# Decode attention in a two-branch decoder step: query rows written at the end of the selection, value matmuls handed out at each column chunk

## The chip, the core and the metric

The kernel runs on one core of one Trainium2 chip. The metric is the device time of one execution in microseconds. The core has a matrix engine (TensorE, PE in the profile, with PEld for its weight loads), VectorE (DVE), ScalarE (ACT), GpSimd (POOL) and SyncE (SP), whose queue issues nearly all DMAs here. Each engine runs its own list of instructions in order; semaphores tie the lists together.

## The reference

One layer of a decoder trunk is computed for a prompt of 1024 rows and for 8 sampled rows (one new token for each of 8 sequences with 4096 cached tokens). One input projection feeds an attention branch and an mLSTM branch, whose gated outputs go through one output projection. The prompt's attention and the mLSTM are left out below; the part that the change touches is the sampled rows' sparse attention: an indexer scores all 4097 positions, the best 256 are taken, and the attention is computed over the gathered keys and values.

```python
scores = indexer_scores(qi, ki_all, wi)                # (8, 1, 4097)
_, idx = lax.top_k(scores, 256)
phys = page_table[idx // 128]; off = idx % 128         # paged cache
kg = where(in_past, cache_k[phys, off], k_new)         # (8, 1, 256, 2, 128)
vg = where(in_past, cache_v[phys, off], v_new)
logits = einsum('bqhgd,bqjhd->bqhgj', q, kg) * 128 ** -0.5
p = softmax(logits)
o = einsum('bqhgj,bqjhd->bqhgd', p, vg)                # 8 heads in 2 groups, 128 wide
```

## The kernel before

**The projection.** `proj` (line 1363) makes the input projection in 61 tiles of 128 columns. All 1032 rows (1024 of the prompt, 8 sampled) are streamed against weights split into a high and a low part (`wH`, `wL`), three matmuls for each of 16 slices of the contraction. A tile goes in four quarters (`q`), each with one weight load of 256 KB (`wraw`, line 210), a cast on ScalarE (line 213) and a subtraction on VectorE (line 214); a quarter has three column chunks of 344 rows, 12 matmuls each (line 1360, `mm`). The three chunks of a tile accumulate in three PSUM banks `pj0`, `pj1`, `pj2`, of which there is one each: the next tile's first matmul on a bank waits until VectorE has evacuated it (line 333, into `ev`).

**The side work.** All else up to tile 58 is written as generators, "jobs", in two lanes (lines 313 to 320). After each quarter, `proj` calls `lane.step`, which lets a job emit its next pieces until a debt of one quarter is covered; a piece's price is its weight (the number that it yields) against the job's weight that is left and the quarters up to the job's end tile. What the jobs emit is not the final order: a scheduler then orders each engine's list by its own model of time, save for instructions that `pin` ties to the written order. In the second lane, `job_dsel` (line 983) selects the 256 positions of each sampled row; it ends with 16 steps of one-hot matmuls (line 1084) that place the chosen indices, which are written to `slotS` and read back as `idxs` (lines 1096, 1097). `job_datt` (line 1192) is the attention itself and starts when the prompt's index job is done (`ix_free`).

**In `job_datt`**, the keys of sequence `b` are gathered in two halves of 128 rows (`gather`, line 1211, by GpSimd). The query rows of all sequences are transposed by `rows` (line 918: eight transposes on TensorE at line 923 into two banks, two copies on VectorE at line 924, one store at line 925) into the DRAM tensor `qrowS`, and `qload` (line 1220) reads one sequence's row back onto all 128 partitions, 512 KB each. For each half VectorE multiplies keys by queries (line 1239, `jk`) and sums (line 1243, `lT`). After a softmax over 64 rows (lines 1249 to 1274) the values are gathered through the same six buffers `kv`, and TensorE forms the output with four small matmuls for each sequence, 128 by 128 against 4 columns (line 1284), into one bank that line 1292 reads.

The tensors of `job_datt` lie in memory that the index job held, whose last act is the store of `biasS` (line 538). When `datt` is done, the prompt's attention (`job_att`, line 541) may start in the first lane.

Of the kernel before, what the change touches and what calls it, by code (L numbers as in the profile page):

```python
# [41 lines left out]
T_AK = 9  # L42
T_AV = 11
T_AQ = 13
# [54 lines left out]
class Lane:  # L99
# [23 lines left out]
    def _ready(self):  # L123
        return bool(self.jobs) and self.jobs[0].start * 4 <= self.now and all(f() for f in self.jobs[0].conds)

    def step(self, now):
        self.now = now
        self.debt -= 1.0
        while self.debt < 0:
            if self.cur is None and not self._ready():  # L130
                self.debt = 0.0
                return
            self.debt += self._next()
# [7 lines left out]
def body(tc, A, stop=None):  # L141
# [36 lines left out]
    dec = fix.tile([128, T_G, NB], F32, name="dec")  # L178
# [4 lines left out]
    def dt_(shape, name):  # L183
        return tc.dram_tile(shape, F32, name=name)
# [15 lines left out]
    def bank(n=512, dt=F32, parts=128):  # L200
        t = psg.tile([128, 512], F32, name="bank")
        return t

    def wload(src, cols, pool, raws, bufs, tag=""):
        raw = pool.tile([128, 4, 128], F32, name="wraw", bufs=raws)
        H = pool.tile([128, 4, 128], F32R, name="wH" + tag, bufs=bufs)
        L = pool.tile([128, 4, 128], F32R, name="wL" + tag, bufs=bufs)

        def load(s, queue=SY):
            return queue.dma_start(raw[:, s, :cols], src[:, s])  # L210

        def cast(s):
            a = SC.copy(H[:, s, :cols], raw[:, s, :cols])  # L213
            return a, V.tensor_tensor(L[:, s, :cols], raw[:, s, :cols], H[:, s, :cols].bitcast(F32), OP.subtract)  # L214

        return H, L, load, cast

    def wsplit(src, cols, pool, raws, bufs, tie=False, tag=""):
        H, L, load, cast = wload(src, cols, pool, raws, bufs, tag)
        dma = load(slice(0, 4))  # L220
        if tie:
            pin(dma)
        cast(slice(0, 4))
        return H, L
# [81 lines left out]
    def chunks(t):  # L306
        return CHQ if T_IQ <= t < T_AK else CH
# [470 lines left out]
    def job_ml():  # L778
        gT = mlc["gT"]
        with tc.tile_pool(name="ml", bufs=2) as pm:  # L780
# [129 lines left out]
            for h in range(4):  # L910
                SY.dma_start(A["C_p"][h], C[:, h, :256])
                SY.dma_start(A["n_p"][h].rearrange("(p o) -> p o", o=1), C[:, h, 256:257])

    slotS = tc.dram_tile([NB, 256], I32, name="slotS")
    krowS = dt_([NB, 1024], "krowS")
    qrowS = dt_([NB, 1024], "qrowS")

    def rows(pool, col, dst):
        vr = pool.tile([NB, 8, 128], F32, name="vr")
        for x in range(2):  # L920
            p = bank().rearrange("p (a b) -> p a b", a=4)
            for y in range(4):
                PE.transpose(p[:NB, y, :], col(x * 4 + y), ident)
            V.tensor_copy(vr[:, x * 4:x * 4 + 4], p[:NB])
        SY.dma_start(dst, vr.rearrange("p a b -> p (a b)"))
# [57 lines left out]
    def job_dsel():  # L983
        NP1 = NPG + 1
        with tc.tile_pool(name="dq", bufs=1, side="right") as pd:
# [78 lines left out]
            V.tensor_scalar(pti2[:, 1], pti[:, 0:256], 15, None, OP.bitwise_and)  # L1064
            V.tensor_copy(ptf, pti2)
            yield 5000
            i16 = cst[:, C_I16:C_I16 + 16].unsqueeze(1).to_broadcast([128, 16, 16])
            ph = bank()
            for b in range(NB):
# [122 lines left out]
    def job_datt():  # L1192
        with tc.tile_pool(name="da", bufs=1, side="right") as pd:
# [13 lines left out]
            def gather(src, b):  # L1207
                out = []
                for u in range(2):
                    g = pd.tile([128, 256], F32, name="kv", bufs=6)  # L1210
                    gi = G.indirect_dma_start(out=g, out_offset=None, in_=A[src],
                                         in_offset=bass.IndirectOffsetOnAxis(ap=idxs[:, b, u:u + 1], axis=0))
                    out.append(g)
                    if not u:
                        pin(gi)
                return out

            def qload(b):
                qb = pd.tile([128, 8, 128], F32, name="qb", bufs=3)
                SY.dma_start(qb.rearrange("p a b -> p (a b)"), qrowS[b].partition_broadcast(128))  # L1220
                return qb

            kgs = [gather("ck", b) for b in range(2)]
            with tc.tile_pool(name="dq", bufs=1, side="right") as pq:
                rows(pq, lambda j: dec[:, T_AQ + j, :], qrowS)
            qbs = [qload(b) for b in range(2)]
            yield 2500
            yield 2500
# [44 lines left out]
            PT = pd.tile([128, 3, 64], F32, name="PT")  # L1273
            V.tensor_copy(PT, p3[:, :192].rearrange("p (a b) -> p a b", a=3))
            yield 4000
            po = bank()
            for b in range(NB):
                if b + 2 < NB:
                    vgs.append(gather("cv", b + 2))
                vg = vgs.pop(0)  # L1280
                for v in range(2):
                    o = b * 8 + v * 4
                    for u in range(2):
                        PE.matmul(po[:, o:o + 4], vg[u][:, v * 128:v * 128 + 128], PT[:, u, o:o + 4],
                                  start=(u == 0), stop=(u == 1))
                yield 2500
            ot = pd.tile([128, 8, NB], F32, name="ot")
            for b in range(NB):
                V.tensor_tensor(kn[:, b, :].rearrange("p (v h) -> p v h", v=2),
# [16 lines left out]
    def ix_weight(blocks):  # L1306
# [6 lines left out]
    lanes = [Lane([Job("gates", T_AK, T_AK + 1.5, 8500, job_gates),  # L1313
                   Job("index", T_AK, 35.5, 3000 + sum(map(ix_weight, groups)), lambda: job_index(groups)),
                   Job("att", T_MQ, 47.75, 2 * 2 * sum(2 * (1 + (i + 1) * 0.5) for i in range(8)) + 6, job_att, att_free),
                   Job("ml", T_G + 11.25, T_PRE, 38, job_ml)]),
             Lane([Job("dscore", T_AK, 18, 16 + 128 + 2, job_dscore),
                   Job("dsel", T_AK, 34, 2000 + 31 * 1700 + 10000 + 16 * 2800 + 2000, job_dsel),
                   Job("datt", T_MQ, 38.5, 7500 + 8 * 5000 + 4000 + 8 * 2500 + 3000, job_datt, ix_free),
                   Job("dml", T_G + 11.25, T_PRE - 0.5, 20000 + 16 * 2500 + 5000, job_dml, dml_free)])]  # L1320
    gateV = gateS.rearrange("(k p) r -> k p r", p=128)
# [16 lines left out]
    def mixmake(ci, k, pool, h, l, tie=False, tmp=None):  # L1338
        c0, cn = CB[ci]
        oo, mr = h.bitcast(F32), l.bitcast(F32)  # L1340
        mx = (tmp or pool).tile([128, cn], F32, name="mx", bufs=2)
        if k < 8:
            v = V.scalar_tensor_tensor(mx, mr, 0.5, oo, OP.mult, OP.mult)
        else:
            v = V.scalar_tensor_tensor(mx, oo, mlw[:, k - 8:k - 7], mr, OP.mult, OP.mult)
        if tie:
            pin(v)
        SC.copy(h, mx)
        V.tensor_tensor(l, mx, h.bitcast(F32), OP.subtract)
        mixb[ci][k] = (h, l)  # L1350

    def wsrc(t, q):
        return A["wm"][q] if t == 0 else A["wa"][t - 1, q]

    def mm(ps, cols, t, q, c, H, L):
        c0, cn = chunks(t)[c]
        for k in range(4):
            kk = q * 4 + k
            for w_, x_, z in ((H, xH, 0), (H, xL, 1), (L, xH, 2)):
                PE.matmul(ps[:cols, :cn], w_[:, k, :cols], x_[kk][:, c0:c0 + cn],  # L1360
                          start=(kk == 0 and z == 0), stop=(kk == 15 and z == 2))

    def proj(ts, hook=None):
        pss = []
        for x, t in enumerate(ts):
            nc_ = len(chunks(t))
            if x:
                pss.append([bank() for c in range(nc_)])
            else:
                pss.append([psj.tile([128, 512], F32, name=f"pj{(t * nc_ + c) % 3}") for c in range(nc_)])  # L1370
        for q in range(4):
            ws = []
            for x, t in enumerate(ts):
                cols = NMISC if t == 0 else 128
                with tc.high_priority():
                    if hook and x == 0:
                        hook(q, ws)
                    elif hook and not q:
                        pass
                    elif x:  # L1380
                        ws.append(wsplit(wsrc(t, q), cols, x0, 2, 4, q == 1))
                    else:
                        ws.append(wsplit(wsrc(t, q), cols, wst, 2, 3))
            for x, t in enumerate(ts):
                cols = NMISC if t == 0 else 128
                H, L = ws[x]
                for c in range(len(pss[x])):
                    mm(pss[x][c], cols, t, q, c, H, L)
            for lane in lanes:
                lane.step(ts[0] * 4 + q)  # L1390
            if len(mids) > 3 or mids and not pend:
                for _ in range(2):
                    mixmake(*mids.pop(0), True)
            for k in pend[:2]:
                mids.append(mixload(0, pend.pop(0), pb0, True))
        return pss
# [19 lines left out]
    pss = proj((0, 1, 2), xhook)  # L1416
# [4 lines left out]
    with tc.tile_pool(name="mp", bufs=1) as mp, tc.tile_pool(name="iqp", bufs=1) as iqp:  # L1421
# [5 lines left out]
        for t in range(3, T_AK):  # L1427
            pss = proj((t,))
# [4 lines left out]
    for t in range(T_AK, NT):  # L1433
# [3 lines left out]
        pss = proj((t,))  # L1437
# [39 lines left out]
    for t in range(KT):  # L1477
# [13 lines left out]
        y = pb.tile([128, cn], F32, name=f"y{t}", bufs=1)  # L1491
# [167 lines left out]
```

## Time and profile before

| | |
|---|---|
| three runs | 2039.61, 2039.86, 2044.28 us; median 2039.86 us |
| the profiled execution | 2039.7 us; span 2037.9 us; granted clock of TensorE 0.998 |
| busy | PE 99%, PEld 96%, DVE 58%, ACT 38%, POOL 12% |
| DMA | 257.08 MB moved, mean 126 GB/s |

The span runs from the first to the last instruction; 1.8 us of the profiled execution lie around it. PE's busy share holds overlapping matmuls whose ends are modelled, so PE's own waits and the distance from one matmul's start to the next say more than the share. Times in the profile count from the start of the span. In `job_datt`'s stretch, key products run from 907 to 956 us and value matmuls from 970 to 988 us.

### The profile page before, as it was taken

The numbers are of one execution on the slowest core, as the hardware profiler recorded it, in microseconds if no ns is written. First come the engines' busy times: TensorE is split into PE (matmuls) and PEld (weight loads), VectorE is DVE, ScalarE is ACT, GpSimd is POOL, SyncE is SP. The second block draws the span as 40 slices with busy tenths as digits, with TensorE's granted clock in tenths as the row PEclk, the third lists the DMA queues.
The fourth block names the chain that finished last, engine by engine and source line by source line (L and its number), as shares of the span: only waits on it lengthen the run. The fifth ranks groups of instructions, "written<-read, shape, count | busy, mean of one in ns | idle before, by whom it ended". The sixth has DMA issues, their size and how long they took to land.

```text
span 2037.9 us, 34353 instructions
## 1 busy us (share of the span) xinstructions
PE 2022.5 (99%) x12678; PEld 1950.9 (96%) x12678; DVE 1182.2 (58%) x2956; ACT 777.7 (38%) x1631; POOL 235.2 (12%) x294
## 2 busy tenths in 40 slices
PE   9999999999999999999999999999999999999998
PEld 8999999999999999999999999999999999998886
DVE  8333367665696876878354554446677466664331
ACT  8121234233631446312255554534444344433222
POOL 0000111100000000023211011012222211111110
PEclk9999999999999999999999999999999999999999
DMA  7444533322222212244323332146675558566212
GB/s 247 106 112 125 154 111 114 100 84 63 76 75 70 75 56 63 64 142 154 120 70 92 110 95 86 48 131 197 207 217 176 152 184 314 174 223 221 81 49 103
DMA packets 203669, 257.08 MB, mean 126 GB/s; under 512 B 39685, under 2 KB 130885, under 8 KB 203501
## 3 DMA queue, kind: packets, MB, share of 16 engines
q1 hardware_dynamic: 198253, 240.82, 38.1%
q0 software_dynamic: 4096, 12.59, 2.0%
q8 instruction: 99, 1.62, 0.3%
q10 hardware_dynamic: 1152, 1.49, 0.2%
q14 instruction: 69, 0.57, 0.1%
HBM read 195.00 MB, written 59.82 MB: 125 GB/s over the span
## 4 chain that ended last, share of the span: by engine, by line
PE 96%; issue 1%; DVE 1%; ACT 1%; DMA 1%; SPq 0%; POOLq 0%; POOL 0%; DVEq 0%
PE pj L1360 62%; PE bank L1487 7%; PE bank L1525 6%; PE pj L1525 4%; PE bank L461 3%; PE bank L656 3%; PE bank L605 3%; PE bank L647 2%; PE bank L968 1%; PE bank L1360 1%; DMA xr<-in_xT_dram 1%; PE bank L845 1%; PE bank L851 1%; PE bank L847 1%; PE bank L1084 0%
## 5 line engine op out<-in xcount | busy, mean ns | idle before, releaser
L1360 PE MATMUL pj<-xH,wH 128*128 128x344 f32 (+2 forms) x2736 | 881.4, 324 | 4.0 <-ACT xH L265 2.1
L1360 PE MATMUL pj<-xH,wL 128*128 128x344 f32 (+2 forms) x2736 | 882.0, 323 | 0.0
L1360 PE MATMUL pj<-xL,wH 128*128 128x344 f32 (+2 forms) x2736 | 881.3, 322 | 0.2 <-DVE xL L266 0.2
L1360 PEld LDWEIGHTS pj<-xH,wH 128*128 128x128 f32 (+1 forms) x2736 | 513.1, 188 | 7.8 <-ACT xH L265 3.4
L1360 PEld LDWEIGHTS pj<-xL,wH 128*128 128x128 f32 (+1 forms) x2736 | 512.8, 187 | 3.1 <-DVE xL L266 1.0
L1360 PEld LDWEIGHTS pj<-xH,wL 128*128 128x128 f32 (+1 forms) x2736 | 513.3, 188 | 2.1
L213 ACT CAST wH<-wraw 128x512 fp32r<-128x512 f32 (+2 forms) x375 | 228.4, 613 | 640.4 <-PE pj L1360 422.7
L214 DVE TENSOR_TENSOR wL<-wraw,wH 128x512 fp32r<-128x512 f32 (+2 forms) x375 | 263.0, 707 | 330.6 <-ACT wH L213 302.4
L510 ACT ACTIVATE eq<-eq 128x512 bf16<-128x512 bf16 (+2 forms) x93 | 78.4, 843 | 114.4 <-DVE eq L509 111.8
L333 DVE TENSOR_TENSOR ev<-pj,rstd 128x344 f32<-128x344 f32 x144 | 73.9, 514 | 70.6 <-PE pj L1360 58.8
L463 ACT ACTIVATE rl<-bank 128x512 f32<-128x512 f32 (+2 forms) x160 | 78.7, 522 | 89.0 <-PE bank L461 63.3
L466 DVE SCALAR_TENSOR_TENSOR s<-rl,wiN,s 128x512 f32<-128x512 f32 (+2 forms) x150 | 94.8, 655 | 27.1 <-ACT rl L463 24.3
L652 DVE TENSOR_TENSOR ptL<-bank,ptH 128x512 fp32r<-128x512 f32 (+1 forms) x80 | 50.5, 635 | 66.9 <-ACT ptH L651 66.2
L1487 PE MATMUL bank<-mL,wH 128*128 128x392 f32 x256 | 87.2, 341 | 0.0
L1487 PE MATMUL bank<-mH,wL 128*128 128x392 f32 x256 | 86.9, 341 | 0.0
L1487 PE MATMUL bank<-mH,wH 128*128 128x392 f32 x256 | 86.6, 341 | 0.0
L461 PE MATMUL bank<-ki,qi 128*128 128x512 f32 (+2 forms) x320 | 76.3, 358 | 0.0
L1525 PE MATMUL bank<-wH,mH 128*128 128x512 f32 x192 | 75.4, 393 | 0.0
L1525 PE MATMUL bank<-wH,mL 128*128 128x512 f32 x192 | 75.2, 392 | 0.0
L1525 PE MATMUL bank<-wL,mH 128*128 128x512 f32 x192 | 75.2, 392 | 0.0
L336 POOL COPY dec<-ev 128x8 f32<-128x8 f32 x28 | 14.1, 505 | 514.9 <-DVE ev L333 262.1
L651 ACT CAST ptH<-bank 128x512 fp32r<-128x512 f32 (+1 forms) x80 | 42.9, 540 | 66.9 <-PE bank L647 63.2
(389 smaller groups left out, 2858.1 us busy)
## 6 DMA issues: line engine op xcount, KB each, us to landing
wraw<-in_wa_dram SPq DMA_DIRECT2D x238, 256.0 KB
wraw<-in_wo_dram SPq DMA_DIRECT2D x64, 256.0 KB
wraw<-in_wt_dram SPq DMA_DIRECT2D x64, 256.0 KB
gateS<-ev SPq DMA_DIRECT2D x72, 172.0 KB
qkv<-mlS SPq DMA_DIRECT2D x16, 512.0 KB
xr<-in_xT_dram SPq DMA_DIRECT2D x15, 516.0 KB
qi<-qS SPq DMA_DIRECT2D x24, 256.0 KB
mlS<-ev SPq DMA_DIRECT2D x48, 128.0 KB
```

The costliest lines, as they stand in the source:

```text
L213: a = SC.copy(H[:, s, :cols], raw[:, s, :cols])
L214: return a, V.tensor_tensor(L[:, s, :cols], raw[:, s, :cols], H[:, s, :cols].bitcast(F32), OP.subtract)
L333: V.tensor_tensor(e, ps[c][:cols, :cn], rstd[:cols, c0:c0 + cn], OP.mult)
L461: PE.matmul(p[:, :cn], qi[:, h % 4, :], ki[x][:, c0:c0 + cn], start=(x == 0), stop=(x == 1))
L463: SC.activation(r[:, :cn], p[:, :cn], AF.Relu)
L466: v = V.scalar_tensor_tensor(s[:, c0:c0 + cn], r[:, :cn], wv, s[:, c0:c0 + cn], OP.mult, OP.add)
L510: SC.activation(junk2[:, :W1], junk2[:, :W1], AF.Copy, accum_out=cnt[:, 1:2])
L605: PE.matmul(p[:, :cn], a_[:, h, :], b_[:, c0:c0 + cn], start=(z == 0), stop=(z == 2))
L656: PE.matmul(oT[:, :256], a_[:, k2 + kk, :], b_[:, ks_], start=(k2 + kk == 0 and z == 0), stop=(k2 + kk == i and z == 2))
L1360: PE.matmul(ps[:cols, :cn], w_[:, k, :cols], x_[kk][:, c0:c0 + cn], start=(kk == 0 and z == 0), stop=(kk == 15 and z == 2))
L1487: PE.matmul(p, w_[:, k, :], x_, start=(n == 0), stop=(n == 47))
L1525: PE.matmul(p, x_[:, bs], w_.rearrange("p a b -> p (a b)"), start=(n == 0 and z == 0), stop=(n == KT - 1 and z == 2))
```

## The change

Two things are changed. First, `rows` for `qrowS`, with its eight transposes, two copies and one store, moves from `job_datt` (behind the first two key gathers) to `job_dsel`, ahead of the 16 one-hot steps, with a yield of its own of 1000, by which `job_dsel`'s weight grows. Second, while the value matmuls are being emitted, the second lane is in a set `fine`; `proj` then steps that lane after each column chunk, with a third of a quarter's debt, and not again at the quarter's end.

```diff
-    def step(self, now):
+    def step(self, now, amount=1.0):
         self.now = now
-        self.debt -= 1.0
+        self.debt -= amount
...
+    fine = set()
...
             V.tensor_copy(ptf, pti2)
             yield 5000
+            with tc.tile_pool(name="dr", bufs=1, side="right") as pq:
+                rows(pq, lambda j: dec[:, T_AQ + j, :], qrowS)
+            yield 1000
...
             kgs = [gather("ck", b) for b in range(2)]
-            with tc.tile_pool(name="dq", bufs=1, side="right") as pq:
-                rows(pq, lambda j: dec[:, T_AQ + j, :], qrowS)
             qbs = [qload(b) for b in range(2)]
...
             yield 4000
+            fine.add(1)
             po = bank()
             for b in range(NB):
...
                 yield 2500
+            fine.discard(1)
...
-                   Job("dsel", T_AK, 34, 2000 + 31 * 1700 + 10000 + 16 * 2800 + 2000, job_dsel),
+                   Job("dsel", T_AK, 34, 2000 + 31 * 1700 + 11000 + 16 * 2800 + 2000, job_dsel),
...
+            done = set()
             for x, t in enumerate(ts):
...
                 for c in range(len(pss[x])):
                     mm(pss[x][c], cols, t, q, c, H, L)
-            for lane in lanes:
-                lane.step(ts[0] * 4 + q)
+                    for y in tuple(fine):
+                        done.add(y)
+                        lanes[y].step(ts[0] * 4 + q, 1.0 / len(pss[x]))
+            for y, lane in enumerate(lanes):
+                if y not in fine and y not in done:
+                    lane.step(ts[0] * 4 + q)
```

## Prediction

> **What bounds the kernel now.** I read the page first, for the bound.
>
> ```profile
> span 2037.9 us, 34353 instructions
> PE 2022.5 (99%) x12678; PEld 1950.9 (96%) x12678; DVE 1182.2 (58%) x2956; ACT 777.7 (38%) x1631; POOL 235.2 (12%) x294
> ...
> PE 96%; issue 1%; DVE 1%; ACT 1%; DMA 1%; SPq 0%; POOLq 0%; POOL 0%; DVEq 0%
> ```
>
> The chain that ends last is TensorE for 96% of the span. A side job then moves the end in two ways alone: it changes how much TensorE must do, or it makes TensorE wait or run slowly. So the second view is TensorE's list of waits over the whole run.
>
> ```profile
> PE pj L1360 <- ACT xH L265: 2.1, 2, 1.4
> PE pj L1360 <- DVE ev L333: 1.2, 1, 1.2
> PE bank L162 <- DVE cmask L157: 1.0, 1, 1.0
> PE bank L255 <- DVE rstd L257: 0.8, 1, 0.8
> PE bank L1360 <- ACT wH L213: 0.8, 1, 0.8
> PE pj L1360 <- DVE mfull L333: 0.7, 1, 0.7
> PE pj L1360 <- DVE xL L266: 0.2, 1, 0.2
> ```
>
> Seven groups, 6.8 us. All but the second belong to lines of the start (loading and splitting the input). The second, one wait of 1.2 us for an evacuation, is the only one in the stretch where the changed program differs: its built lists equal those of before up to about 640 us of this trace, and on TensorE again from tile 46 on, with the same instructions on each engine. The third view is that stretch by windows.
>
> ```profile
> 640.00:892.00 252.00, 252.00 (x1746) 242.29 (x1745) 189.82 (x477) 107.90 (x195) 4.19 (x9) 1.00 0.23 65
> 892.00:1000.00 108.00, 106.78 (x687) 105.53 (x686) 66.85 (x102) 21.30 (x40) 39.70 (x40) 0.98 0.53 169
> 1000.00:1360.00 360.00, 360.00 (x2449) 353.85 (x2448) 179.39 (x576) 177.19 (x433) 29.63 (x32) 1.00 0.29 88
> ```
>
> Columns are the window, its length, busy time of PE, PEld, DVE, ACT and POOL, granted clock, DMA share and GB/s. TensorE is idle for 1.22 us in the middle window and never in the others, and the clock is below 1.00 there alone. Both losses lie in the decode attention, so they are all that this change can win in its own stretch: 1.2 us and a clock dip priced below. Both together are far under 0.3% of the time, which is 6.1 us and about what a measurement of this kernel can tell from no change.
>
> **The idle time, step by step.** The timelines of TensorE, VectorE and SyncE show how it arises.
>
> ```profile
> 914.88 0.32 PE L1360 MATMUL pj<-xL,wH 128*128 128x344 f32 x1
> 915.04 0.31 PE L1360 MATMUL pj<-xH,wL 128*128 128x344 f32 x1
> 916.57 0.39 PE L1360 MATMUL pj<-xH,wH 128*128 128x344 f32 x1 [1.22 <-DVE ev L333]
> ```
>
> ```profile
> 899.57 0.35 DVE L1198 TENSOR_TENSOR c<-cntp,cst 64x64 f32<-64x64 f32 x2 [4.18 <-issue]
> 899.84 1.27 DVE L924 COPY vr<-bank 8x512 f32<-8x512 f32 x2
> 907.51 1.26 DVE L1239 TENSOR_TENSOR jk<-kv,qb 128x1024 f32<-128x1024 f32 x1 [4.65 <-DMA qb<-qrowS]
> ...
> 915.92 0.51 DVE L333 TENSOR_TENSOR ev<-pj,rstd 128x344 f32<-128x344 f32 x1
> ```
>
> ```profile
> 896.29 0.45 SPq L538 DMA_DIRECT2D biasS<-gt  x1
> 899.54 0.48 SPq L1203 DMA_DIRECT2D bias<-in_cst_dram  x1
> 901.14 0.29 SPq L925 DMA_DIRECT2D qrowS<-vr  x1
> 903.02 0.33 SPq L1220 DMA_DIRECT2D qb<-qrowS  x1
> ```
>
> At 899.5 the memory becomes free and the decode attention starts; VectorE copies the query rows, SyncE stores them, loads them back at 903.02, and the first product starts at 907.51 after a wait of 4.65. The products are pinned, so the evacuation of the finished tile stands behind the first of them and begins at 915.92, ends at 916.43; TensorE, which would have gone on at 915.20 (one pitch of 0.16 after 915.04), starts at 916.57.
>
> **Part one, the query rows.** It removes the two copies and the store from that chain and puts them some 200 us earlier. In the changed list the loads of `qb` stand right behind the load of `bias`. The time at which the memory is free stays the next thing that is late. It moves a little: the built VectorE list now has a weight subtraction (line 214) ahead of line 529, and that one must wait for a cast.
>
> ```profile
> 886.47 0.81 DVE L529 TENSOR_SCALAR gt<-s,sm 128x1024 bf16<-128x1024 f32 x1 [1.77 <-DMA biasS<-gt]
> 886.60 0.62 ACT L213 CAST wH<-wraw 128x512 fp32r<-128x512 f32 x1 [5.04 <-PE pj L1360]
> ```
>
> The cast ends at 887.22, so line 529 starts up to 1.4 us later (0.7 for the wait, 0.7 for the subtraction), and an evacuation moved ahead may add as much; the store of `biasS` queued at 896.29 behind the evacuated tile's stores, which hide most of it. I take 0.5 (ends 0 and 2). Then `bias` is issued at 900.0, the first `qb` 0.5 later at 900.5, and with the 4.49 us from 903.02 to 907.51 the first product starts at 905.0, which is 2.5 earlier.
>
> ```profile
> L1239 DVE TENSOR_TENSOR jk<-kv,qb 128x1024 f32<-128x1024 f32 x16 | 19.6, 1224 | 5.0 <-DMA qb<-qrowS 4.7
> L924 DVE COPY vr<-bank 8x512 f32<-8x512 f32 x4 | 2.6, 670 | 0.0
> L923 PE MATMUL bank<-cst,dec 128*8 128x128 f32 x12 | 2.0, 272 | 0.0
> ```
>
> In the changed list one product more (1.22) stands ahead of the evacuation. It takes 8.41 us from 907.51 to 915.92, plus 1.22, plus 0.51 for itself: 905.0 + 10.1 is 915.1, and TensorE follows 0.14 later, at 915.3, against 915.20. The wait falls from 1.22 to about 0.1. **Gain 1.1 us**, between 1.4 and, with the memory 2 us late and the extra product, a loss of 0.3.
>
> The moved step itself: its eight transposes are 8 of the 12 of the last row, some 1.3 us of TensorE. They are in both lists (the scheduler had hoisted them ahead of their copies before, too). Cost 0; they would cost 1.3 only if they were new. The two copies (1.3 us of VectorE) now stand between the evacuations of a tile's first and second chunk, at about 700 us by their neighbours in the list, where VectorE is busy for 190 of 252 us. Behind them wait that evacuation and TensorE's next tile. If nothing covered them TensorE would lose 1.3. I take 0, since in the 252 us of that window no evacuation made TensorE wait at all. The store to `qrowS` goes past some 75 entries of SyncE's queue and stands there ahead of the second chunk's stores and the next weight load; it waits for the copies, which precede what those stores wait for anyway, so 0 (bound 1.3, not to be added twice). On GpSimd the first gathers still follow line 1198's release; nothing moves.
>
> **Part two, the value matmuls.** The lane's debt gives three sequences to one quarter, one to each chunk, then two and two, in place of three at the quarter's end. But the built list of TensorE hardly notices: its first 12 value matmuls still stand next to each other, and the other 20 still go in groups of one and three, between 59 other rows in both lists, for the softmax and the gathers decide when they are ready. So the cost of switching between the two kinds of matmul stays, and so does this:
>
> ```profile
> 970.02 2.74 PE L1284 MATMUL bank<-PT,kv 128*128 128x4 f32 x24
> ...
> 974.00 0.49 PE L1360 MATMUL pj<-xL,wH 128*128 128x344 f32 x1
> 974.28 0.49 PE L1360 MATMUL pj<-xH,wL 128*128 128x344 f32 x1
> ...
> 977.15 0.42 PE L1360 MATMUL pj<-xH,wH 128*128 128x344 f32 x1
> 977.40 0.31 PE L1360 MATMUL pj<-xL,wH 128*128 128x344 f32 x1
> ```
>
> ```profile
> 972.00:974.00 2.00, 2.00 (x16) 0.98 0.66 201
> 974.00:976.00 2.00, 2.00 (x8) 0.50 0.53 168
> 976.00:978.00 2.00, 2.00 (x11) 0.66 0.35 113
> ```
>
> After 12 matmuls (24 passes) with 4 columns each, granted clock falls to 0.50 and the pitch rises to 0.29. From 974.00 to 977.40 there are 12 steps, which at 0.16 would take 1.9 instead of 3.4: the dip costs 1.5 us. As the burst stays, I price part two at 0, with ends of -1.5 (no dip) and +1.5 (one more, if a group lands badly).
>
> The Trainium skill, "TensorE: Matmul & The Clock Gate", section "Part 1: The HAM clock gate", has the clock halve after an idle window of about 3.4 us. Taken literally it speaks against the second part: TensorE is not idle here, so there would be no dip to remove; the trace contradicts it with 0.50 behind 2.74 us of busy but narrow matmuls.
>
> **The sum.** 2039.7 for the profiled execution, less 1.1, is 2038.6; the median of the runs, 2039.86, less 1.1, is 2038.8. I say 2038.7.
>
> **The rivals.** *The dip goes too.* The burst's shape is the same, but it starts some tenths earlier or later against whatever samples it. Then 2038.7 - 1.5 = 2037.2. For it: the dip occurs once in 2037.9 us although the 16 matmuls of a one-hot step stand together 16 times in the first window without one, so it sits near a threshold. Against: the same 24 passes. The same section of the Trainium skill calls the window free-running and its effect variable from run to run, which would make this rival a matter of the execution and not of the change. Chance 0.25.
>
> *Nothing happens*, because the first product waits for the memory or the gathered keys rather than for the queries, and starts about 906.3, where the extra product makes the evacuation as late as before: 2039.8. Chance 0.12.
>
> *Slower: the evacuation falls further behind.* The three 512 KB loads of `qb` now go out together, ahead of two weight loads that stood between them. If they hold each other up and the first product starts at 907.5 as before, the evacuation ends 1.22 later than before: 2039.7 + 1.2 = 2040.9. The rival decides from 906.3 on, and each microsecond later costs one. To pass 6.1 us the first product would have to start after 912.4, or the weights arrive so late that a second tile stalls. For it: DMA is at 0.53 in that window, 4 MB of queries in it. Against: the first `qb` load came within 4.5 us before, beside gathers and a weight load. The Trainium skill, "Trainium Kernel Development and Optimization", section "Key Constraints", says that all queues share the same 16 DMA engines and interleave; it is on this rival's side, and no run shows here how strongly. Chance 0.16, half of it beyond 0.3%.
>
> **How the numbers follow.** The forecast has 0.47, the rivals 0.25, 0.12 and 0.16. Only a slowdown can pass 0.3%, since all that can be won is 1.4 + 1.5 us. Faster by over 0.3%: 0.02, for what the trace doesn't show; slower by over 0.3%: 0.08; within: 0.90. The range reaches from 2036.0 (the dip gone and the bound of part one, with a little less around the span) to 2043.0 (the slower rival with 2 us more, and runs of before up to 2044.28).
>
> **What would show it.** Right: in the changed profile no or a 0.1 us wait of TensorE for `ev` near 916 us; the first product at about 905 without a wait on the query rows' store; 24 passes of value matmuls in one piece and a dip behind them. Wrong: a wait for `ev` over 1.3 us, waits of TensorE for `wH` or `wL` between 900 and 960, a second window with a clock under 1.00, or a copy of `vr` with an idle TensorE behind it near 700 us.

## The result and the profile after

The changed kernel takes 2045.61 us (median of 14 runs, 2042.85 to 2047.65), the kernel before on the same chip 2040.38 us (median of 14). The ratio is 1.0023, with a 95% interval from 1.0016 to 1.0029: 0.23% slower, where 1.1 us of gain was forecast. That is under the 0.3% named as about what a measurement can tell from no change, but with 14 runs of each the interval excludes 1.0000, and the time lies above the range given. The profiled execution of after takes 2047.65 us, which is the slowest of its 14; its span is 7.7 us longer than that of before, where the medians lie 5.2 us apart.

The page of after, first the span and the busy times, then the head of the chain that ended last:

```profile
span 2045.6 us, 34337 instructions
PE 2027.3 (99%) x12678; PEld 1955.8 (96%) x12678; DVE 1183.8 (58%) x2956; ACT 778.6 (38%) x1631; POOL 232.5 (11%) x294
...
PE 96%; DMA 2%; DVE 1%; issue 1%; ACT 0%; SPq 0%; POOLq 0%; POOL 0%; DVEq 0%
```

TensorE still carries the chain, but the share of DMA has risen from 1% to 2%. TensorE's list of waits in after has one line that grew, the first of these two (before: 1.2 us, one time):

```profile
PE pj L1364 <- DVE ev L333: 5.8, 2, 3.9
PE pj L1364 <- ACT xH L265: 0.9, 1, 0.9
```

So there are two waits for an evacuation, 1.9 and 3.9 us. The windows that the prediction used say where; columns as there:

```profile
640.00:892.00 252.00, 252.00 (x1746) 242.41 (x1745) 189.18 (x477) 108.21 (x195) 4.46 (x9) 1.00 0.24 67
892.00:1000.00 108.00, 106.08 (x673) 105.01 (x672) 65.33 (x102) 20.59 (x39) 37.64 (x40) 0.97 0.50 158
1000.00:1360.00 360.00, 356.10 (x2412) 349.65 (x2411) 177.99 (x570) 174.53 (x426) 29.39 (x32) 1.00 0.29 88
```

The second window lost 1.92 us where it lost 1.22, and the third, which lost nothing before, lost 3.90. The third lies 350 us behind anything that the diff touches. Finer windows of after show what follows each wait:

```profile
914.00:916.00 2.00, 1.13 (x8) 0.85 (x6) 2.00 (x3) 0.62 (x1) 0.71 (x1) 1.00 0.46 160
916.00:918.00 2.00, 0.95 (x5) 0.98 (x6) 2.00 (x4) 0.00 (x0) 0.94 (x1) 0.93 0.58 172
918.00:920.00 2.00, 2.00 (x8) 2.00 (x8) 2.00 (x5) 0.00 (x0) 0.14 (x1) 0.50 0.91 258
920.00:922.00 2.00, 2.00 (x11) 2.00 (x11) 1.97 (x4) 0.00 (x0) 1.00 (x2) 0.72 0.90 238
...
1342.00:1344.00 2.00, 0.94 (x6) 0.65 (x5) 0.11 (x1) 0.00 (x0) 0.00 (x0) 1.00 0.71 225
1344.00:1346.00 2.00, 0.00 (x0) 0.00 (x0) 1.97 (x5) 1.60 (x3) 1.29 (x1) 1.00 0.06 14
1346.00:1348.00 2.00, 1.15 (x7) 1.15 (x8) 1.88 (x5) 1.28 (x2) 1.68 (x2) 0.95 0.63 201
1348.00:1350.00 2.00, 2.00 (x9) 2.00 (x9) 1.74 (x6) 1.99 (x8) 1.18 (x2) 0.50 0.17 54
1350.00:1352.00 2.00, 2.00 (x11) 2.00 (x11) 1.05 (x4) 0.34 (x1) 0.00 (x0) 0.70 0.63 193
```

Behind each wait the granted clock falls to 0.50, and a 2 us window holds 8 or 9 matmuls instead of 14 or 15. Two microseconds times what the clock lacks, summed, is 0.14 + 1.00 + 0.56 = 1.7 us for the first stretch and 0.10 + 1.00 + 0.60 = 1.7 for the second. The account for the profiled pair: 0.7 more idle time and 1.7 of clock at 916, 3.9 and 1.7 at 1343, 8.0 together against a span 7.7 longer; the third dip, behind the value matmuls, is in both profiles. These are one execution of each kernel; what the others show of the waits and the dips stands in the table further down.

**The wait at 916 us.** VectorE in after:

```profile
906.77 1.23 DVE L1241 TENSOR_TENSOR jk<-kv,qb 128x1024 f32<-128x1024 f32 x1 [4.30 <-DMA kv<-in_ck_dram,idxs]
...
915.26 1.22 DVE L1241 TENSOR_TENSOR jk<-kv,qb 128x1024 f32<-128x1024 f32 x1
916.40 0.51 DVE L333 TENSOR_TENSOR ev<-pj,rstd 128x344 f32<-128x344 f32 x1
```

The first product waits for gathered keys, not for queries, and starts at 906.77, only 0.74 earlier than before. One more product stands ahead of the evacuation, which comes at 916.40, 0.48 later than in the profile of before. On GpSimd and SyncE in after stand the reasons: the gather of the first keys, and the three loads of `qb` that go out at the same time.

```profile
900.23 0.97 POOL L1215 DMA_INDIRECT kv<-in_ck_dram,idxs  x1 [4.77 <-DVE kn L1246]
```

```profile
899.85 2.53 SPq L1224 DMA_DIRECT2D qb<-qrowS  x3
```

**The wait at 1343 us.** VectorE in after, and the part of the chain that leads to it (start, length, what):

```profile
1333.74 0.52 DVE L333 TENSOR_TENSOR ev<-pj,rstd 128x344 f32<-128x344 f32 x1 [0.75 <-PE pj L1364]
...
1336.47 0.51 DVE L333 TENSOR_TENSOR ev<-pj,rstd 128x344 f32<-128x344 f32 x1
...
1343.89 0.23 DVE L1117 TENSOR_TENSOR gi<-gi,bb 128x64 f32<-128x64 f32 x1 [5.21 <-DMA bb<-in_bg_dram]
...
1346.28 0.51 DVE L333 TENSOR_TENSOR ev<-pj,rstd 128x344 f32<-128x344 f32 x1
```

```profile
1334.95 8.82 DMA bb<-in_bg_dram
```

The third evacuation of a tile stands behind an addition of the sampled rows' mLSTM job (`gi`, line 1117), which waits for a load of 4 KB that took 8.8 us, and behind 2.2 us of other work that VectorE does next. The same place in before:

```profile
1331.38 0.52 DVE L333 TENSOR_TENSOR ev<-pj,rstd 128x344 f32<-128x344 f32 x1 [0.78 <-PE pj L1360]
1333.90 0.52 DVE L333 TENSOR_TENSOR ev<-pj,rstd 128x344 f32<-128x344 f32 x1 [2.01 <-PE pj L1360]
...
1335.99 0.52 DVE L333 TENSOR_TENSOR ev<-pj,rstd 128x344 f32<-128x344 f32 x1
...
1350.08 0.23 DVE L1113 TENSOR_TENSOR gi<-gi,bb 128x64 f32<-128x64 f32 x1 [3.02 <-DMA bb<-in_bg_dram]
```

There all three evacuations are done before the addition, which waits without harm. (The load is slow there too: asked for at 1343.06, it has landed by 1350.08, 7.0 us later. No run shows how long it takes with nothing ahead of it.) What moved is the end of the prompt's attention: its last store goes out on SyncE at 1327.96 in after, 5.78 ahead of the tile's first evacuation, and at 1333.68 in before, 2.30 behind it. Behind that store, two mLSTM jobs start together, with two loads of 512 KB and two of 256 KB (1.5 MB):

```profile
1327.96 0.37 SPq L698 DMA_DIRECT2D attS<-ob  x1
...
1330.60 0.43 SPq L797 DMA_DIRECT2D qkv<-mlS  x1
```

```profile
1333.68 0.37 SPq L698 DMA_DIRECT2D attS<-ob  x1
...
1336.50 0.42 SPq L797 DMA_DIRECT2D qkv<-mlS  x1
```

(the first fence is SyncE in after, the second in before). The burst that fell behind the evacuations now falls 8.1 us earlier against the tile, on top of them.

### The profile page after: what moved, and what is told of

Same layout as the page of the kernel before. It is cut to its first block, busy times and chain, and to the rows that moved or that the text cites. A ratio compares the mean times of both kernels' runs of the same rounds, so it can differ in the third digit from the quotient of the medians.

```text
span 2045.6 us, 34337 instructions
## 1 busy us (share of the span) xinstructions
PE 2027.3 (99%) x12678; PEld 1955.8 (96%) x12678; DVE 1183.8 (58%) x2956; ACT 778.6 (38%) x1631; POOL 232.5 (11%) x294
## 3 DMA queue, kind: packets, MB, share of 16 engines
q8 instruction: 99, 1.62, 0.3%
## 4 chain that ended last, share of the span: by engine, by line
PE 96%; DMA 2%; DVE 1%; issue 1%; ACT 0%; SPq 0%; POOLq 0%; POOL 0%; DVEq 0%
PE pj L1364 62%; PE bank L1496 7%; PE bank L1534 6%; PE pj L1534 4%; PE bank L461 3%; PE bank L656 3%; PE bank L605 3%; PE bank L647 2%; PE bank L969 1%; PE bank L1364 1%; DMA xr<-in_xT_dram 1%; PE bank L845 1%; PE bank L851 1%; PE bank L847 1%; DMA bb<-in_bg_dram 0%
```

## The experiments

### Each half alone

The kernel after without the finer stepping, and the kernel after with the rows put back, which leaves the finer stepping alone; both diffs against after:

```diff
             yield 4000
-            fine.add(1)
...
-            fine.discard(1)
```

> Only the query rows are moved; the value matmuls are handed out at each step of a quarter as before. Its instructions stand on every engine in the order of the kernel after. Theory (all of the loss comes from the moved rows: TensorE waits for an evacuation near 916 us and again near 1343 us, and each wait is followed by a stretch at half clock): as after, ratio to before 1.002 to 1.003, TensorE's waits for ev sum to 5.5 to 6 us. Rival (the finer handing out costs the 5 us): ratio 1.000, waits for ev as before, 1.2 us.

```diff
-            with tc.tile_pool(name="dr", bufs=1, side="right") as pq:
-                rows(pq, lambda j: dec[:, T_AQ + j, :], qrowS)
-            yield 1000
...
             kgs = [gather("ck", b) for b in range(2)]
+            with tc.tile_pool(name="dq", bufs=1, side="right") as pq:
+                rows(pq, lambda j: dec[:, T_AQ + j, :], qrowS)
...
-   Job("dsel", ..., 2000 + 31 * 1700 + 11000 + ...
+   Job("dsel", ..., 2000 + 31 * 1700 + 10000 + ...
```

> Only the finer handing out of the value matmuls; the rows stay with the first loads. Its instructions stand in the order of the kernel before. Theory: no difference, ratio 0.999 to 1.001, waits for ev 1.2 us, the dip behind the first 24 value passes as before. Rival (the finer handing out costs the time): ratio 1.002 to 1.003.

Rows alone: 2045.86 us, ratio 1.0025 (1.0016 to 1.0034). Finer stepping alone: 2040.94 us, ratio 1.0005 (0.9995 to 1.0014). TensorE's wait for `ev` in the two profiles:

```profile
PE pj L1362 <- DVE ev L333: 4.7, 2, 3.3
```

```profile
PE pj L1363 <- DVE ev L333: 1.6, 1, 1.6
```

The whole loss comes from the rows. The finer stepping does nothing, as its unchanged order of instructions says; the dip behind the value matmuls is missing in its profile, of which more below. The waits are 0.8 to 1.3 us less (rows) and 0.4 more (stepping) than I expected: a wait differs by some tenths between executions of the same program.

### The gate bias added later

```diff
-            for _ in range(4):
+            for _ in range(7):
                 yield 2000
             pin(V.tensor_tensor(gi, gi, bb...
```

> The kernel after, with the addition of the gate bias (gi, which waits 5.21 us for bb) asked for three steps later, so that it stands behind the third evacuation of the tile near 1343 us and not ahead of it. Theory: the wait of 3.9 us there goes and with it the half-clock stretch behind it (1347 to 1351, about 1.5 us); the wait of 1.9 us near 916 and its stretch stay. Span 2045.6 - 5.4 = 2040.2, ratio to before 1.0005 to 1.0015. Rival A (a wait costs its idle time alone, the low clock behind it has another cause): span 2041.7, clock still low at 1347 to 1351. Rival B (something else is late there as well, such as the queues' loads): the wait for ev stays over 2 us and the span over 2043.

2043.24 us, ratio 1.0013 (1.0004 to 1.0022); the span of the profiled execution is 2039.3. The ratio is where the theory had it, but for another reason: the wait only shrank, from 3.9 to 2.45 us, as rival B had it (its bound on the span did not hold), and the profile has no dip at all. (At 2041.06 us it is the fastest of the 11 runs, so the others may well have dips.) Its VectorE and GpSimd:

```profile
1341.51 0.52 DVE L333 TENSOR_TENSOR ev<-pj,rstd 128x344 f32<-128x344 f32 x1 [5.56 <-POOL ev L390]
```

```profile
1340.55 0.92 POOL L390 TENSOR_TENSOR ev<-ev 128x344 f32<-128x344 f32 x1 [12.88 <-DMA ev<-gateS]
```

With the addition out of the way, the evacuation waits for a buffer that GpSimd frees, and GpSimd for a gate tile that SyncE had asked for at 1332.56, behind the burst. `bb` was only the last of several loads that the burst held up. So the order of one addition is not the cause; whatever stands ahead of the evacuation waits for loads behind the burst.

### Without the step behind the rows

```diff
                 rows(pq, lambda j: dec[:, T_AQ + j, :], qrowS)
-            yield 1000
...
-   Job("dsel", ..., 2000 + 31 * 1700 + 11000 + ...
+   Job("dsel", ..., 2000 + 31 * 1700 + 10000 + ...
```

> The kernel after, without the step of weight 1000 behind the moved rows and with the job's weight as before. The built order then has three score products ahead of the evacuation near 916 us, as before has, where after has four; the order near 1343 us stays that of after. Theory (the order at 916 decides, not the start of the first product): first product still near 906.8 us, the wait for ev there at most 1.2 us and the clock behind it 1.00, the wait of 3.9 us near 1343 us stays: span 2045.6 - 2.2 = 2043.4, down to 2042.9, ratio 1.0015 to 1.0025. Rival (the late keys decide): the wait near 916 stays at 1.9 us with its low clock, span 2045.6.

2044.59 us, ratio 1.0018 (1.0009 to 1.0027). The three products and the wait near 916:

```profile
907.53 1.23 DVE L1240 TENSOR_TENSOR jk<-kv,qb 128x1024 f32<-128x1024 f32 x1 [4.86 <-DMA kv<-in_ck_dram,idxs]
...
915.91 0.50 DVE L333 TENSOR_TENSOR ev<-pj,rstd 128x344 f32<-128x344 f32 x1
```

```profile
916.56 0.40 PE L1363 MATMUL pj<-xH,wH 128*128 128x344 f32 x1 [0.80 <-DVE ev L333]
...
1343.00 0.66 PE L1363 MATMUL pj<-xH,wH 128*128 128x344 f32 x1 [3.15 <-DVE ev L333]
```

The first product starts 0.76 later than in after, and yet the wait falls from 1.92 to 0.80 with the clock at 1.00 behind it: one product fewer ahead of the evacuation is worth more. The wait near 1343 stays, and the attention's last store is 5.78 us ahead of the tile's first evacuation as in after (1324.87 and 1330.65), so it is the moved rows and not the job's weight that shifted it; by what path through the scheduler was not followed. The theory holds for the two waits, though not for the start of the first product; the gain in time, 0.0005 of the ratio, lies inside the intervals.

### One query row for all sequences

```diff
-            qbs = [qload(b) for b in range(2)]
+            q0 = qload(0)
+            qbs = [q0, q0]
...
-                    qbs.append(qload(b + 2))
+                    qbs.append(q0)
```

> The kernel after, in which all eight sequences take the query rows of the first: one load of 512 KB where there are eight. It leaves out the other seven. Theory (the gathered keys land 6.5 us after their issue because three loads of query rows share the DMA engines with them): the first product starts at 904 to 905 us, when the one load has landed. Rival (a gather takes this long by itself): the first product starts at 906.5 to 907 us as in the kernel after, waiting for the keys, with the DMA share at 904 to 906 well under 1.

Its one run took 2045.96 us, as after does. In its profile, GpSimd, then VectorE:

```profile
901.38 0.98 POOL L1215 DMA_INDIRECT kv<-in_ck_dram,idxs  x1 [4.91 <-DVE kn L1247]
```

```profile
905.68 1.23 DVE L1242 TENSOR_TENSOR jk<-kv,qb 128x1024 f32<-128x1024 f32 x1 [2.10 <-DMA kv<-in_ck_dram,idxs]
...
915.31 0.51 DVE L333 TENSOR_TENSOR ev<-pj,rstd 128x344 f32<-128x344 f32 x1
```

The gathers start 1.15 us later in this execution. From the first gather to the first product it takes 4.30 us, where after took 6.54 (900.23 to 906.77): the two loads of queries that are gone had cost the keys 2.2 us in this pair. In all eight profiles with the moved rows and every query load, this stretch takes 5.8 to 7.1 us, so 1.5 to 2.8 longer than with one load. The product still waits for the keys, so the theory's mechanism holds and its reason for the start (the query load) does not. Four products stand ahead of the evacuation here too, and TensorE does not wait for it at all. So the wait near 916 takes both, the additional product and the late keys: without the one it falls to 0.80, without the other to nothing. The wait near 1343 is 3.61, and with the dips it is what keeps this run as slow as after.

### After once more

> The kernel after once more, unchanged, for a second profile of it. Theory (the half-clock stretches behind a wait of 1.4 to 3.9 us come in some executions and not in others): waits for ev 4.5 to 6 us as before, and the stretches of clock 0.50 at 916 to 922, 974 to 978 and 1345 to 1351 not all three as in the first profile. Rival (they follow from the program alone): the same three stretches.

One run, 2046.62 us, span 2044.8. The waits are 1.58 and 3.86, and the first has no dip behind it, nor do the value matmuls. Behind the second the clock is low for twice as long as in the first profile:

```profile
1344.00:1346.00 2.00, 1.01 (x3) 1.01 (x4) 2.00 (x4) 0.99 (x1) 2.00 (x3) 0.54 0.54 202
1346.00:1348.00 2.00, 2.00 (x8) 2.00 (x8) 1.18 (x6) 1.82 (x7) 0.40 (x1) 0.50 0.15 55
1348.00:1350.00 2.00, 2.00 (x8) 2.00 (x8) 1.13 (x4) 0.62 (x1) 0.00 (x0) 0.50 0.82 257
1350.00:1352.00 2.00, 2.00 (x11) 2.00 (x11) 0.00 (x0) 0.00 (x0) 1.67 (x2) 0.76 0.04 6
```

That is 0.92 + 1.00 + 1.00 + 0.48 = 3.4 us. The same program has other dips in another execution.

### Four key buffers

If the burst near 1340 is the cause, a kernel with the rows moved whose attention ends where it did before must be free of that wait. Four buffers for `kv` instead of six happen to build such an order.

```diff
-   g = pd.tile([128, 256], F32, name="kv", bufs=6)
+   g = pd.tile([128, 256], F32, name="kv", bufs=4)
```

> The kernel after with four buffers for gathered keys and values instead of six, which makes the gathers wait for buffers and brings the built order near 1340 us (loads of the attention's successors behind the first two evacuations of the tile) back to that of before, though the rows stay moved; four products still stand ahead of the evacuation near 916 us. Theory (the moved rows end the attention job about 8 us earlier against the projection's tiles, so that its successors' burst of loads of 1.5 MB falls on an evacuation): the wait near 1343 us goes altogether, not only the 1.5 us that moving the gate bias took away; the wait of 1.3 to 1.9 us near 916 stays: waits for ev 1.3 to 2 us in sum, ratio to before 1.000 to 1.001. Rival (the moved rows load the queues there whatever the order): waits for ev over 3.5 us, ratio over 1.0013.

> Four key buffers, and the moved rows without the step of weight 1000 behind them and with the job's weight as before: three products ahead of the evacuation near 916 us and the loads near 1340 us behind the evacuations. Theory: waits for ev 0.8 to 1.2 us in sum, as before or less; ratio 0.9993 to 1.0005. Rival (the moved rows cost more than the two waits): ratio over 1.001. Rival (what was forecast, a gain of 1.1 us): waits for ev 0.1 us, ratio 0.9995.

From after (rows moved, with the step): 2040.36 us, ratio 0.9997 (0.9988 to 1.0006). Without the step as well: 2038.84 us, ratio 0.9991 (0.9982 to 1.0000). In the first, SyncE and VectorE near 1333, and the one wait that is left:

```profile
1333.38 0.37 SPq L698 DMA_DIRECT2D attS<-ob  x1
```

```profile
1331.01 0.52 DVE L333 TENSOR_TENSOR ev<-pj,rstd 128x344 f32<-128x344 f32 x1 [0.70 <-PE pj L1364]
```

```profile
PE pj L1364 <- DVE ev L333: 1.3, 1, 1.3
```

The attention's last store is again 2.37 us behind the tile's first evacuation, the wait near 1343 is gone altogether, and with it the loss: 1.0023 has become 0.9997. The rival (the moved rows load the queues whatever the order) falls.

Four buffers change one thing more. The value matmuls that stand in one piece are 16 passes instead of 24 (first this kernel, then after):

```profile
970.55 1.84 PE L1287 MATMUL bank<-PT,kv 128*128 128x4 f32 x16
```

```profile
971.85 2.73 PE L1287 MATMUL bank<-PT,kv 128*128 128x4 f32 x24
```

In none of the four profiles with four buffers does a dip follow them. The dip is worth 1.7 us where it comes, so a part of what four buffers gain may be this and not the order near 1340; the wait that went with its dip, 4.9 us and more, is the larger part.

### The same buffers in before, and the best version again

> The kernel before with four buffers for gathered keys and values instead of six; the rows stay with the first loads. Theory (four buffers do nothing by themselves but shift the built order, and the small gain of the moved rows without the step comes from the evacuation near 916 us): wait for ev near 916 us 1.2 to 1.6 us as in before, none near 1340 us, ratio 0.9995 to 1.0005. Rival (the four buffers themselves are the gain): ratio 0.9993 or less.

> Four key buffers and the moved rows without the step, once more, to narrow the interval beside the kernel before with four buffers on the same chip. Theory: wait for ev 0.8 us, ratio 0.9985 to 0.9998. Rival (its first ratio was chance): 0.9998 to 1.0008.

Before with four buffers: 2040.95 us, ratio 0.9993 (0.9984 to 1.0002), waits for `ev` of 1.57 us near 916 and 1.0 near 1358. That is at the rival's bound, and its interval doesn't decide between the two; the shorter piece of value passes would be one way in which the buffers gain by themselves. The rows moved without the step, with four buffers: 2039.12 us, ratio 0.9981 (0.9972 to 0.9990), beside 0.9991 the first time; TensorE's wait near 916 is 0.19 us in this profile. The two times of this version differ little (2038.84 and 2039.12); before was slower on the second chip (2042.22 against 2040.06). On the same chip it is 1.8 us below before with four buffers (2040.95 - 2039.12; 0.6 to 3.1 us by the spread of the 11 runs of each), and that fits the profiled waits, 2.6 us in sum against 0.19 here and 0.82 the first time. This version beats both kernels, against before by 0.1 to 0.2%; the first interval just reaches 1.0000, the second stays under it. So with the evacuations spared, the moved rows do gain something like what was forecast; what the buffers bring by themselves is open.

## Why the prediction was wrong

**Where to look (failed).** The step that failed is the third view: "its built lists equal those of before up to about 640 us of this trace, and on TensorE again from tile 46 on", and from it, that both losses in the decode attention "are all that this change can win in its own stretch". I took a stretch that ends with tile 46, found no idle time between 1000 and 1360 us in before, and read that as nothing to lose. But an idle time of zero in before says nothing on how near a wait is. The order of VectorE's and of SyncE's instructions differs up to about 1356 us, the attention ends 8.1 us earlier against the tile, and 3.3 to 3.9 us of idle time and 1.7 to 3.4 of clock behind it were lost there. The slower rival looked to the first product ("would have to start after 912.4") or to late weights that stall a second tile; a second tile did stall, but 430 us later, and for an evacuation.

**The first product (mis-sized).** Forecast 905.0, 2.5 earlier than before, from the landing of `qb`; measured 906.77, waiting for keys. Executions of one kernel shift by up to a microsecond here, so the start is best counted back from the point at which TensorE would have gone on without the wait. That point is 915.13 and 916.12 in the two profiles of after. The first product lies 7.4 to 7.8 us ahead of it in the three executions with before's order near 916, and 8.4 to 9.0 ahead in the five with after's four products and all query loads. By the means that is 1.2 earlier and no more, which is just what the additional product takes, and so the wait is 1.22 to 1.62 in the three and 1.26 to 1.92 in the five. The forecast gain of 1.1 did not come, and the 0.7 lost in the profiled pair is within what executions differ by. The rival "nothing happens" named this, the gathered keys and the evacuation "as late as before"; the slower rival named the three loads that hold each other up. With three products ahead of the evacuation (no step) the wait was 0.80, 0.82 and 0.19.

**How strongly loads hold each other up.** The Trainium skill, "Trainium Kernel Development and Optimization", section "Key Constraints", has all queues share 16 DMA engines. The prediction said that no run showed how strongly; the runs now do: two more loads of 512 KB put 1.5 to 2.8 us on 4.3 (one profile with the single load, eight with all).

**The memory, the moved step.** The first instruction on the freed memory (line 1202 in after) started at 899.35 in the first profile of after, and at 899.6 to 900.5 in the others with moved rows: 0.5 was a fair size. The copies near 700 us cost nothing: PE is busy for all 252.00 us of the first window, as forecast.

**Part two (right, within the interval).** Priced at 0, and measured alone at 1.0005 (0.9995 to 1.0014), which is 1.0 us less to 2.9 us more.

**The dip (open to chance).** "The dip stays" was no property of the program. Over the twelve profiled executions (idle time in us from TensorE's waits; loss is 2 us times the lacking clock, summed over 2 us windows; a low clock behind the run's last matmul, where TensorE has nothing left to do, is in every profile and is not counted):

| kernel | wait near 916 | loss | loss near 975 | wait near 1343 | loss |
|---|---|---|---|---|---|
| before | 1.22 | 0 | 1.7 | none | 0 |
| finer stepping alone | 1.62 | 0 | 0 | none | 0 |
| before, four buffers | 1.57 | 0 | 0 | none | 0 |
| after | 1.92 | 1.7 | 1.7 | 3.90 | 1.7 |
| after once more | 1.58 | 0 | 0 | 3.86 | 3.4 |
| rows alone | 1.41 | 0 | 1.7 | 3.26 | 1.7 |
| gate bias later | 1.32 | 0 | 0 | 2.45 | 0 |
| no step | 0.80 | 0 | 0 | 3.15 | 1.7 |
| one query | none | 0 | 1.7 | 3.61 | 3.4 |
| four buffers | 1.26 | 0 | 0 | none | 0 |
| four buffers, no step | 0.82 | 0 | 0 | none | 0 |
| the same again | 0.19 | 0 | 0 | none | 0 |

Behind each of the five waits of 3.15 us and more the clock fell; behind the wait of 2.45 it did not, behind the eleven near 916 us once (1.92); behind the 24 narrow passes in four executions of the eight that have them in one piece, and never behind the 16 of the four executions with four buffers. So a wait of 3.15 to 3.9 us cost 4.9 to 7.3 us, and the forecast 1.5 us for the value matmuls' dip was its size where it came (1.7), not its mean (half of that). That "the dip occurs once in 2037.9 us" held for one execution, not for the kernel.

## What to carry to other kernels

When a change moves work in a program whose order a scheduler sets, compare the built lists to the end of their differences, on every engine, and look at each place where a new job starts: which loads go out there, and which evacuation or buffer release stands within their landing time, even if nothing waits there now. "No idle time" in a profile says nothing about the margin, so measure it (the evacuation's start against the next tile's first matmul). A wait of TensorE of over 3 us cost about one and a half to two times its length here, since the clock fell behind it.

## What the runs showed of the hardware

In the middle of these runs, loss of clock comes in pieces of 1.7 us, which is 3.4 us at half clock, or two of them. The Trainium skill, "TensorE: Matmul & The Clock Gate", section "Part 1: The HAM clock gate", has a free-running window of about 3.4 us over which TensorE's activity is judged; the size of the pieces and their coming and going between executions agree with it. That a whole window must be idle doesn't agree: waits of 3.15 and 3.26 us sufficed, one of 1.92 us did once, and 24 narrow busy passes did four times. Behind the last matmul the clock fell after 1.8 to 4.6 us in the twelve profiles.

A load of 4 KB (`bb`) took 8.8 us to land behind 1.5 MB of other loads, and the first gathered keys took 1.5 to 2.8 us longer beside three loads of 512 KB than beside one.
